# A decoder layer on one core: split weights 128 bytes into longer tiles, decay ahead of the last head's sums, the MLP norm applied late

## The chip, the core and the metric

The kernel runs on one core of a Trainium2 chip. A core has a matmul engine (PE; its weight loads are shown beside it as PEld), a vector engine (DVE), a scalar engine (ACT), a general engine (POOL) and a sync engine (SP) that here only issues transfers. Every engine takes its own instructions strictly in the order in which the program issues them to it, and waits on semaphores for the others. Data lies in SBUF (128 partitions); matmuls write PSUM, of which this kernel has eight buffers of 128x512 fp32. The metric is the device time of one launch in microseconds (us).

## The reference

One layer of an autoregressive decoder for 512 tokens of width 1024, all in fp32:

```python
h = rmsnorm(x, ln1);  hq, hk, hv, hr, ha, hatt, hgate = split(h @ w_in)
log_a = log_sigmoid(ha @ w_a2 + b_a) / 16                 # decay of the gated linear attention
o = gla_mixer(hq, hk, hv, log_a)                          # 4 heads, chunks of 64
y_gla = (norm(o) * gla_gn * silu(hr)) @ w_o_gla
o_att = merge of 3 dilated attention groups, 4 heads each # softmax over the groups' sums
x = x + (sigmoid(g_gla) * y_gla + sigmoid(g_att) * (o_att @ w_o_attn)) @ w_out
x = x + square(relu(rmsnorm(x, ln2) @ w_mlp1)) @ w_mlp2   # 1024 -> 4096 -> 1024
x = x + sigmoid(rmsnorm(x, ln3) @ w_pg) * (p @ w_pp)
return rmsnorm(x, ln_f)
```

## The kernel before

**Split operands.** A matmul runs in the rounded type fp32r, one pass. To keep fp32 precision, every operand is split into `hi` (rounded, written by ACT) and `lo` (the rest, `w - hi`, written by DVE), and a product becomes three matmuls: hi·hi, hi·lo, lo·hi. A weight arrives by DMA as a raw tile of 128x1024 (pool `wst`, 6 buffers), ACT writes its `hi` (L226) and DVE its `lo` (L221) into the pool `wsp` (5 and 4 buffers); `fetch` keeps this two or three operands ahead of the matmuls. Everything else of size 128x512 lies in one arena `ar` of `NU` = 69 tiles, `ur` when of type fp32r and `u` otherwise. All tiles of `wst`, `wsp` and `ar` have sizes that are multiples of 512 bytes, and all slices used as matmul operands begin at multiples of 512 bytes in their tile.

**Seven-product groups.** Most projections (23 groups of 512 output columns, `strassen`) are done by a scheme of seven products in place of eight on 2x2 blocks: a stage per product, 24 matmuls with 256 moving columns each. The weight combinations S1 to S4 come by DMA with accumulation (POOL) and two DVE sums (L206, L212). In groups of kind `quad` the weights are the stationary operand, in `quadt` the moving one. The other weights (kinds `fm`, `tm`, `half`) are used with 512 moving columns. Per group, four results are finished by an ACT copy at the block's beginning and a DVE addition at its end.

**An order by hand.** PE's stream sets the order. `run` issues matmuls in pieces of eight and calls `step` after each. `step` takes one closure of the list `later` (finishing work, splits), and, each time `pace` moving columns have gone by, resumes one generator of the list `side`, of which the first two take turns (`WAYS` = 2). `drain` runs both lists empty with no matmuls of the main stream between.

**Where the change touches.**

- Behind the group `v0`, `pace` is set to 2560; `side` gets `pv(0)` to `pv(3)` (the weighted sums of the attention heads) and behind them `decay()` (four small products, Abs, Exp, Ln on ACT, a subtraction L817 and a prefix scan L818 on DVE for each head). They run beside the groups `gq`, `gk`, `gv0`; then `drain()`, then the linear attention `gla(0)`, `gla(1)` beside the four `oa` weights.
- Ahead of the MLP, `rms_gen(acc1, norm2, 6, 2)` waits six steps, sums squares over partitions with four one-column matmuls (L377), takes the inverse root on POOL (L364, L365), makes a diagonal matrix of it (L390), splits that, and spreads it over partitions by two matmuls (L396, L397). The result `norm2[1]` is multiplied into each hidden block together with the relu (L1167), ahead of the square (L1176).
- Each half of the second MLP product ends with four additions from PSUM into `xx` (L1226); `normed` then makes the split operands of the last norm and its sum of squares. Behind them, `pp` and `pg` run with tokens on the output partitions.
- The last token tile of `pg1` is done in two halves of 256 columns, each followed by `gated`: sigmoid (L1267), product (L1268), sum (L1269), sum of squares (L1270); `scale_out` and `put` write the output.

Of the kernel before, what the change touches and what calls it, by code (L numbers as in the profile page):

```python
# [11 lines left out]
F32R = mybir.dt.float32r  # L12
I32 = mybir.dt.int32
AF = mybir.ActivationFunctionType
OP = mybir.AluOpType
# [4 lines left out]
P = 128  # L20
T = 512
D = 1024
KC = D // P
EPS = 1e-6
# [14 lines left out]
QUADS = ("quad", "quadt")  # L39
# [54 lines left out]
UNITS = weight_units()  # L94
# [32 lines left out]
C_LN2, C_LN3, C_BA, C_GN, C_LN1, C_LO, C_N = 0, 8, 16, 20, 28, 36, 38  # L127
W0, W12 = 384, 256

NU, NW, PIECE, WAYS = 69, 5, 8, 2  # L130

NRAW = 6

NWARM = 8

# [2 lines left out]
def block_kernel(ctx, tc, xT, ws, pT, wts, wha, wa2, vec, lnf, rel, onehot, ident_d, mask_d, out):  # L138
# [13 lines left out]
    def u32(name="u"):  # L152
        return ar.tile([P, T], F32, tag="u", name=name)
# [4 lines left out]
    def mmt():  # L158
        return mm.tile([P, T], F32, tag="mm", name="mmt")
# [19 lines left out]
    def drain():  # L179
        while side or later:  # L180
            step()
# [20 lines left out]
    def sums(i):  # L202
# [7 lines left out]
        elif what == "S4":  # L210
            w = raw[f"{q}.S4"] = raw[f"{q}.S2"]
            V.tensor_tensor(w, w, raw[f"{q}.A12"], op=OP.add)  # L212

    def fetch(upto):

        while done[0] < min(upto, len(OPERANDS) - 1):
            i = done[0] = done[0] + 1
            if i >= 0:
                w, hi = ready[OPERANDS[i]]
                lo = wsp.tile([P, 1024], F32R, tag="lo", name="lo", bufs=NW - 1)  # L220
                V.tensor_tensor(lo, w, hi.bitcast(F32), op=OP.subtract)  # L221
                ready[OPERANDS[i]] = (hi, lo)
            if 0 <= i + 1 < len(OPERANDS):
                w = raw[OPERANDS[i + 1]]
                hi = wsp.tile([P, 1024], F32R, tag="hi", name="hi", bufs=NW)
                S.activation(hi, w, AF.Copy)  # L226
                ready[OPERANDS[i + 1]] = (w, hi)
            if 0 <= i + 2 < len(OPERANDS):
                sums(i + 2)
            if 0 <= i + 3 < len(OPERANDS):  # L230
                prepare(i + 3)
# [5 lines left out]
    def run(mms, n=PIECE, shared=False):  # L237
        for i in range(0, len(mms), n):
            for o, l, r, a, b in mms[i:i + n]:
                TE.matmul(o, lhsT=l, rhs=r, start=a, stop=b, skip_group_check=shared)  # L240
            step(PIECE * r.shape[-1])
# [8 lines left out]
    def cols(t, c):  # L250
        return t[0][:, c], t[1][:, c]
# [28 lines left out]
    def halves(t):  # L280
        return slice(t * HT, (t + 1) * HT)
# [79 lines left out]
    def rsqrt(r, ms, n):  # L361

        v = st.tile([P, n], F32, tag=f"rv{n}", name="rv", bufs=4)
        V.tensor_scalar(v, ms, EPS, None, op0=OP.add)  # L364
        GP.tensor_tensor(r, v, mh[:, 0:n], op=OP.pow)  # L365
# [4 lines left out]
        S.activation(t, x, AF.Square, scale=1.0 / 32.0)  # L370
        return t

    def rms_tok(acc):

        ps = smt()
        for i in range(4):
            TE.matmul(ps[:, i:i + 1], lhsT=acc[:, i * P:(i + 1) * P], rhs=ones[:, 0:1], start=True, stop=True)  # L377
        r = const.tile([P, 4], F32, name="rtok", bufs=3)
        rsqrt(r, ps[:, 0:4], 4)
        return r  # L380

    def rms_gen(acc, res, wait=0, gap=0):

        for _ in range(wait):
            yield
        r = rms_tok(acc[0])
        for _ in range(gap):
            yield
        dg = u32()
        V.tensor_tensor(dg.rearrange("p (a b) -> p a b", a=4), ident[:, None, :].to_broadcast([P, 4, P]),  # L390
                        r[:, :, None].to_broadcast([P, 4, P]), op=OP.mult)
        dh, dl = split(dg)
        for _ in range(2 + gap):
            yield
        pb = smt()
        TE.matmul(pb, lhsT=ones_r, rhs=dh, start=True, stop=False)  # L396
        TE.matmul(pb, lhsT=ones_r, rhs=dl, start=False, stop=True)  # L397
        bc = const.tile([P, T], F32, tag="rstd", name="rstd", bufs=2)
        S.activation(bc, pb, AF.Copy)
        res += [r, bc, pb]  # L400
# [586 lines left out]
    side.append(weights())  # L987
    v0 = values("v0")
    drain()
    pace[0] = 2560  # L990
    side.extend(pv(h) for h in range(4))
    side.append(decay())
    gq = heads("gq", HD_SCALE)
    gk = heads("gk", 1.0)
    gv = [values("gv0", True)]
# [152 lines left out]
        later.extend(x1_tile(j))  # L1148
    while len(later) > 5:
        step()  # L1150
    side.append(rms_gen(acc1, norm2, 6, 2))


    hid = [None] * 32
# [4 lines left out]
    def quad(q):  # L1159


        def finish(m, t, s, ps):
            add(m, s, s, ps)

            def scale():
                o = s.rearrange("p (n t) -> p n t", n=2)
                V.scalar_tensor_tensor(out=o, in0=o, scalar=0.0,  # L1167
                                       in1=norm2[1][:, None, halves(t)].to_broadcast([P, 2, HT]),
                                       op0=OP.max, op1=OP.mult)

            def act():
                for n in range(2):
                    j = 4 * q + 2 * n + m
                    if hid[j] is None:
                        hid[j] = u32()
                    S.activation(hid[j][:, halves(t)], s[:, halves(n)], AF.Square)  # L1176

            later.extend([scale, act])

        def extra(i):  # L1180
            if i in (3, 4):
                later.append(lambda: hid_split(i - 3))

        strassen(f"m1q{q}", x1_op, finish, extra=extra if q == 7 else None)
# [6 lines left out]

    for q in range(8):
        quad(q)
        if q == 0 and not norm2:
            drain()
    for k in (2, 3):
        hid_split(k)
    drain()
# [2 lines left out]
    for sub in range(2):  # L1201
        pss = [mmt() if sub == 0 else smt() for _ in range(4)]
        for kk in range(16):
            wh, wl = weight(f"m2s{sub}.{kk}")
            mms = []
            for k in (2 * kk, 2 * kk + 1):
                xh, xl = hs.pop(k)
                for o in range(4):
                    c = slice((k % 2) * 512 + o * P, (k % 2) * 512 + (o + 1) * P)
                    mms += [(pss[o], wh[:, c], xh, k == 0, False), (pss[o], wh[:, c], xl, False, False),  # L1210
                            (pss[o], wl[:, c], xh, False, k == 31)]
            run(mms)
            for k in (2 * kk + 4, 2 * kk + 5):
                hid_split(k if k < 32 or sub else k - 32)
            if sub == 1 and kk == 8:
                for k in range(2):
                    t = u32()
                    GP.dma_start(t, pT[k * P:(k + 1) * P, :])
                    pt.append(split(t))
                for g in range(2):  # L1220
                    t = u32()
                    GP.dma_start(t, lnf[:, g * 512:(g + 1) * 512].to_broadcast([P, 512]))
                    lnb.append(t)
        for o in range(4):
            j = 4 * sub + o
            V.tensor_tensor(xx[j], xx[j], pss[o], op=OP.add)  # L1226
            normed(j, C_LN3, x2s, acc2)
    while later:
        step()
# [30 lines left out]
    sp2 = const.tile([P, 4], F32, name="sp2")  # L1260
    fr = const.tile([P, 4], F32, name="fr")

    def gated(ps, i, c, tt, col):

        n = c.stop - c.start
        sg = u32()
        S.activation(sg[:, 0:n], ps[:, 0:n], AF.Sigmoid, scale=rt3[0][:, tt:tt + 1])  # L1267
        V.tensor_tensor(sg[:, 0:n], sg[:, 0:n], pps[i][:, c], op=OP.mult)  # L1268
        V.tensor_tensor(x2t[i][:, c], x2t[i][:, c], sg[:, 0:n], op=OP.add)  # L1269
        S.activation(sg[:, 0:n], x2t[i][:, c], AF.Square, scale=1.0 / 32.0, accum_out=ss2[:, col:col + 1])  # L1270

    def evac_pg0(tt, ps):
        if len(x2t) < 8:
            drain()
        gated(ps, tt, slice(0, 512), tt, tt)
        V.tensor_scalar(sp2[:, tt:tt + 1], ss2[:, tt:tt + 1], EPS, None, op0=OP.add)
        V.tensor_tensor(x2t[tt], x2t[tt], lnb[0], op=OP.mult)

    def scale_out(tt, col):

        V.tensor_scalar(sp2[:, tt:tt + 1], ss2[:, col:col + 1], sp2[:, tt:tt + 1], None, op0=OP.add)
        GP.tensor_tensor(fr[:, tt:tt + 1], sp2[:, tt:tt + 1], mh[:, 0:1], op=OP.pow)
        o = u32()
        S.activation(o, x2t[tt], AF.Copy, scale=fr[:, tt:tt + 1])
        S.dma_start(out[tt * P:(tt + 1) * P, 0:512], o)

    def put(tt, c):
        n = c.stop - c.start
# [3 lines left out]
        SY.dma_start(out[tt * P:(tt + 1) * P, 512 + c.start:512 + c.stop], o[:, 0:n])  # L1292

    def evac_pg1(tt, ps):
        gated(ps, 4 + tt, slice(0, 512), tt, 4 + tt)
        scale_out(tt, 4 + tt)
        put(tt, slice(0, 512))

    tmaj("pg0", x2s, evac_pg0)
    tmaj("pg1", x2s, evac_pg1, tts=range(3))  # L1300
    tok = slice(3 * P, 4 * P)
    for f in range(2):
        c = slice(f * 256, (f + 1) * 256)
        ps = mmt()
        run(three(ps[:, 0:256], [(cols(x2s[k], tok), cols(ready[f"pg1.{k // 2}"], slice((k % 2) * 512 + c.start, (k % 2) * 512 + c.stop)))
                                 for k in range(KC)]))
        gated(ps, 7, c, 3, 8 + f)
        if f == 0:
            V.tensor_scalar(sp2[:, 3:4], ss2[:, 8:9], sp2[:, 3:4], None, op0=OP.add)
    scale_out(3, 9)  # L1310
    put(3, slice(256, 512))
    put(3, slice(0, 256))
# [85 lines left out]
```

## Time and profile before

| | us |
|---|---|
| median of 3 runs (989.91 to 991.78) | 990.1 |
| the profiled execution: its own time | 991.5 |
| its span, first to last instruction | 989.7 |
| PE busy in the span | 973.7 |
| DVE, ACT, POOL busy | 689.4, 520.9, 94.4 |

The profiled execution is 1.8 us longer than its span and 1.4 us longer than the median of the runs. In the profile's rows, a line number is that of the code before; names follow the program (`mmt` and `smt` are the two sets of four PSUM buffers). A matmul's reported duration (about 280 ns for 256 columns) is longer than the distance to the next one, since they are pipelined; what a matmul costs is read from a stretch of the chain: time divided by count.

### The profile page before, as it was taken

What the parts mean: (1) busy time and instruction counts of PE and PEld (TensorE: products, weight loads), DVE (VectorE), ACT (ScalarE), POOL (GpSimd) and SP (SyncE); (2) the same over time, 40 slices, a digit from 0 to 9 for tenths busy, and PEclk for the clock granted to TensorE, in tenths of its full rate; (3) what the DMA queues carried; (4) which work ended last, traced back from release to release, by engine and by line L of the source; (5) the groups of instructions that cost most, each with busy time, mean ns of one, the idle gap of its engine ahead of it and who ended that gap; (6) DMA issues with size and microseconds to landing.
All of it is one profiled execution on the core that took longest, in us unless ns stands there. A gap on an engine that the chain in (4) does not pass through costs nothing.

```text
span 989.7 us, 15873 instructions
## 1 busy us (share of the span) xinstructions
PE 973.7 (98%) x6372; PEld 889.3 (90%) x6372; DVE 689.4 (70%) x966; ACT 520.9 (53%) x875; POOL 94.4 (10%) x136
## 2 busy tenths in 40 slices
PE   9999999999998999999999999999999999999996
PEld 7788999999996999999988889999998888888885
DVE  7777579676579669977955697788778445653554
ACT  7335546445575667565733446555665335442633
POOL 0230011320010021013010001010000000000000
PEclk9999999999999999999999999999999999999999
DMA  8473564974264545455636426656544332523102
GB/s 308 126 205 100 128 147 112 266 202 115 80 157 131 160 98 149 121 146 171 171 92 206 126 46 164 177 131 169 154 145 131 104 96 77 167 88 106 43 1 85
DMA packets 40026, 133.63 MB, mean 135 GB/s; under 512 B 5203, under 2 KB 6815, under 8 KB 39952
## 3 DMA queue, kind: packets, MB, share of 16 engines
q1 hardware_dynamic: 27504, 92.51, 28.5%
q0 software_dynamic: 10720, 36.96, 18.4%
q10 hardware_dynamic: 1728, 3.15, 0.8%
q8 instruction: 50, 0.82, 0.3%
q14 instruction: 24, 0.20, 0.1%
HBM read 126.26 MB, written 8.17 MB: 136 GB/s over the span
## 4 chain that ended last, share of the span: by engine, by line
PE 92%; DVE 3%; issue 2%; ACT 1%; POOL 0%; POOLq 0%; DVEq 0%; ACTq 0%
PE mmt L240 73%; PE smt L240 9%; PE smt L829 1%; DVE lo L221 1%; PE smt L769 1%; PE smt L695 1%; PE mmt L454 1%; PE mmt L453 1%; PE mmt L455 1%; PE smt L875 1%; DVE u L818 0%; PE smt L877 0%; PE smt L428 0%; PE smt L665 0%; PE smt L786 0%
## 5 line engine op out<-in xcount | busy, mean ns | idle before, releaser
L240 PE MATMUL mmt<-ur,hi 128*128 128x256 f32 (+1 forms) x2784 | 608.5, 314 | 1.8 <-ACT u L1002 1.5
L240 PEld LDWEIGHTS mmt<-ur,hi 128*128 128x128 f32 x2784 | 459.9, 191 | 34.3 <-issue 1.9
L240 PE MATMUL mmt<-ur,lo 128*128 128x256 f32 (+1 forms) x1392 | 437.4, 314 | 0.5 <-DVE lo L221 0.5
L221 DVE TENSOR_TENSOR lo<-w,hi 128x1024 fp32r<-128x1024 f32 x236 | 286.2, 1220 | 119.6 <-PE mmt L240 64.2
L226 ACT ACTIVATE hi<-w 128x1024 fp32r<-128x1024 f32 x236 | 246.8, 1053 | 137.1 <-issue 64.0
L240 PEld LDWEIGHTS mmt<-ur,lo 128*128 128x128 f32 x1392 | 266.0, 191 | 16.3 <-DVE lo L221 0.7
L240 PE MATMUL mmt<-hi,ur 128*128 128x256 f32 (+1 forms) x736 | 154.5, 306 | 0.0
L337 ACT ACTIVATE ur<-u 128x512 fp32r<-128x512 f32 x136 | 79.9, 621 | 95.2 <-DVE u L1066 30.9
L240 PEld LDWEIGHTS mmt<-hi,ur 128*128 128x128 f32 x736 | 119.4, 191 | 5.6
L240 PE MATMUL mmt<-lo,ur 128*128 128x256 f32 (+1 forms) x368 | 112.4, 305 | 0.0
L345 DVE TENSOR_TENSOR ur<-u,ur 128x512 fp32r<-128x512 f32 x135 | 89.0, 686 | 20.3 <-ACT ur L337 19.7
L330 DVE TENSOR_TENSOR u<-u,mmt 128x512 f32<-128x512 f32 (+1 forms) x92 | 58.0, 654 | 39.0 <-PE mmt L240 37.4
L240 PE MATMUL smt<-ur,hi 128*128 128x512 f32 x272 | 83.7, 389 | 0.0
L312 ACT ACTIVATE u<-mmt 128x512 f32<-128x512 f32 x92 | 54.4, 592 | 49.7 <-PE mmt L240 49.7
L240 PEld LDWEIGHTS mmt<-lo,ur 128*128 128x128 f32 x368 | 70.2, 191 | 2.7
L240 PEld LDWEIGHTS smt<-ur,hi 128*128 128x128 f32 x272 | 51.1, 188 | 10.6
L240 PE MATMUL smt<-ur,lo 128*128 128x512 f32 x136 | 53.0, 390 | 0.0
L209 POOL DMA_DIRECT2D w<-in_wts_dram x23 | 20.1, 875 | 289.8 <-DVE w L206 210.5
L1176 ACT ACTIVATE u<-u 128x256 f32<-128x256 f32 x64 | 23.0, 409 | 37.2 <-DVE u L1167 37.2
L198 POOL DMA_DIRECT2D w<-in_wts_dram x23 | 20.4, 886 | 202.4 <-DMA w<-in_wts_dram 84.6
L240 PEld LDWEIGHTS smt<-ur,lo 128*128 128x128 f32 x136 | 25.5, 188 | 5.3
L212 DVE TENSOR_TENSOR w<-w 128x1024 f32<-128x1024 f32 x23 | 28.2, 1225 | 0.8
(203 smaller groups left out, 718.2 us busy)
## 6 DMA issues: line engine op xcount, KB each, us to landing
w<-in_wts_dram SPq DMA_DIRECT2D x167, 512.0 KB, 4.0
w<-in_wts_dram POOLq DMA_DIRECT2D x46, 512.0 KB, 5.5
u<-in_xT_dram SPq DMA_DIRECT2D x8, 256.0 KB, 4.7
v_dram<-u POOLq DMA_DIRECT2D x8, 256.0 KB, 6.2
u<-v_dram POOLq DMA_DIRECT2D x8, 256.0 KB, 7.3
y_dram<-u ACTq DMA_DIRECT2D x8, 256.0 KB, 2.4
u<-y_dram POOLq DMA_DIRECT2D x8, 256.0 KB, 7.3
u<-in_xT_dram POOLq DMA_DIRECT2D x8, 256.0 KB, 8.1
```

Of the source, the lines that this page charges most:

```text
L198: GP.dma_start(w, wts[UNIT[f"{q}.A22"]], accum_op=OP.add)
L209: GP.dma_start(w, wts[UNIT[f"{q}.A21"]], accum_op=OP.add)
L212: V.tensor_tensor(w, w, raw[f"{q}.A12"], op=OP.add)
L221: V.tensor_tensor(lo, w, hi.bitcast(F32), op=OP.subtract)
L226: S.activation(hi, w, AF.Copy)
L240: TE.matmul(o, lhsT=l, rhs=r, start=a, stop=b, skip_group_check=shared)
L312: S.activation(sums[c], bank[b], AF.Copy, scale=-scale if c[0] else scale)
L330: V.tensor_tensor(out, s, ps, op=OP.subtract if m else OP.add)
L337: S.activation(hi, x, AF.Copy)
L345: V.tensor_tensor(lo, x, hi.bitcast(F32), op=OP.subtract)
L453: TE.matmul(q0ps[i], lhsT=hi[:, c], rhs=xh, start=k == 0, stop=False)
L1176: S.activation(hid[j][:, halves(t)], s[:, halves(n)], AF.Square)
```

## The change

- **Weight tiles.** `hi` and `lo` tiles are 1152 elements long instead of 1024 (4608 bytes). Operands of the seven-product groups use elements 32 to 1055, so they begin 128 bytes into the tile; the others use elements 0 to 1023.
- **Room.** The arena has 71 tiles instead of 69; the DMA scratch of the POOL queue is set to 8192 bytes (the default in the program before is 16384).
- **Decay.** The order of `side` is `pv(0)`, `pv(1)`, `pv(2)`, `decay()`, `pv(3)`, and `pace` stays at 2048 columns.
- **MLP norm.** `rms_gen` waits 30 steps instead of 6 (gap 4 instead of 2) and computes 1/(mean square + eps) with a DVE reciprocal: since relu(x·r)² = r²·relu(x)², the factor is no longer needed in the hidden blocks (L1167 becomes a maximum with 0) and is multiplied into the PSUM result behind the second product, one more DVE operation for each of the eight output tiles.
- **Last tile.** The last token tile of `pg1` is cut into 384 and 128 columns; both sigmoids are issued ahead of the first part's sum of squares. The first three output transfers of the first half go by SP's queue instead of ACT's.

```diff
-NU, NW, PIECE, WAYS = 69, 5, 8, 2
+NU, NW, PIECE, WAYS = 71, 5, 8, 2
+PAD, SHIFT = 128, 32
+LAST = 384
...
+    def split_weights(tag, i, bufs):
+
+        t = wsp.tile([P, 1024 + PAD], F32R, tag=tag, name=tag, bufs=bufs)
+        o = SHIFT if OPERANDS[i] not in UNIT or UNITS[UNIT[OPERANDS[i]]][1] in QUADS else 0
+        return t[:, o:o + 1024]
...
-                lo = wsp.tile([P, 1024], F32R, tag="lo", name="lo", bufs=NW - 1)
+                lo = split_weights("lo", i, NW - 1)
...
-                hi = wsp.tile([P, 1024], F32R, tag="hi", name="hi", bufs=NW)
+                hi = split_weights("hi", i + 1, NW)
...
-        rsqrt(r, ps[:, 0:4], 4)
+        if squared:
+            V.tensor_scalar(r, ps[:, 0:4], EPS, None, op0=OP.add)
+            V.reciprocal(r, r)
+        else:
+            rsqrt(r, ps[:, 0:4], 4)
...
-    pace[0] = 2560
-    side.extend(pv(h) for h in range(4))
-    side.append(decay())
+    side.extend([pv(0), pv(1), pv(2), decay(), pv(3)])
...
-    side.append(rms_gen(acc1, norm2, 6, 2))
+    side.append(rms_gen(acc1, norm2, 30, 4, True))
...
-            def scale():
-                o = s.rearrange("p (n t) -> p n t", n=2)
-                V.scalar_tensor_tensor(out=o, in0=o, scalar=0.0,
-                                       in1=norm2[1][:, None, halves(t)].to_broadcast([P, 2, HT]),
-                                       op0=OP.max, op1=OP.mult)
+            def positive():
+                V.tensor_scalar(s, s, 0.0, None, op0=OP.max)
...
-            V.tensor_tensor(xx[j], xx[j], pss[o], op=OP.add)
+            t = u32()
+            V.tensor_tensor(t, pss[o], norm2[1], op=OP.mult)
+            V.tensor_tensor(xx[j], xx[j], t, op=OP.add)
             normed(j, C_LN3, x2s, acc2)
...
-        S.dma_start(out[tt * P:(tt + 1) * P, 0:512], o)
+        (S if tt == 3 else SY).dma_start(out[tt * P:(tt + 1) * P, 0:512], o)
...
-    for f in range(2):
-        c = slice(f * 256, (f + 1) * 256)
-        ps = mmt()
...
-        gated(ps, 7, c, 3, 8 + f)
-        if f == 0:
-            V.tensor_scalar(sp2[:, 3:4], ss2[:, 8:9], sp2[:, 3:4], None, op0=OP.add)
+    parts, sgs = [slice(0, LAST), slice(LAST, 512)], []
+    for c in parts:
+        ps, n = mmt(), c.stop - c.start
...
+        sgs.append(gate(ps, n, 3))
+        if c.start == 0:
+            gated(sgs[0], 7, c)
+    squares(sgs[0], 7, parts[0], 8)
+    gated(sgs[1], 7, parts[1])
+    V.tensor_scalar(sp2[:, 3:4], ss2[:, 8:9], sp2[:, 3:4], None, op0=OP.add)
+    squares(sgs[1], 7, parts[1], 9)
     scale_out(3, 9)
...
-    nc = _bacc.Bacc("TRN2", target_bir_lowering=False, num_devices=1)
+    nc = _bacc.Bacc("TRN2", target_bir_lowering=False, num_devices=1, dynamic_dma_scratch_size=8192)
```

More of the change, by code (lines that the diff above doesn't have):

```diff
@@ L371, in square, with rms_tok @@
         return t
-    def rms_tok(acc):
+    def rms_tok(acc, squared=False):
         ps = smt()
@@ L378, in rms_tok, with rms_gen @@
         r = const.tile([P, 4], F32, name="rtok", bufs=3)
-        rsqrt(r, ps[:, 0:4], 4)
+        if squared:
[3 more added lines that the diff above has]
+            rsqrt(r, ps[:, 0:4], 4)
         return r
-    def rms_gen(acc, res, wait=0, gap=0):
+    def rms_gen(acc, res, wait=0, gap=0, squared=False):
         for _ in range(wait):
             yield
-        r = rms_tok(acc[0])
+        r = rms_tok(acc[0], squared)
         for _ in range(gap):
@@ L1176, in act @@
                     S.activation(hid[j][:, halves(t)], s[:, halves(n)], AF.Square)
-            later.extend([scale, act])
+            later.extend([positive, act])
         def extra(i):
@@ L1193, in block_kernel @@
         quad(q)
-        if q == 0 and not norm2:
-            drain()
     for k in (2, 3):
@@ L1261, in block_kernel, with gate, gated, squares @@
     fr = const.tile([P, 4], F32, name="fr")
-    def gated(ps, i, c, tt, col):
-        n = c.stop - c.start
+    def gate(ps, n, tt):
         sg = u32()
         S.activation(sg[:, 0:n], ps[:, 0:n], AF.Sigmoid, scale=rt3[0][:, tt:tt + 1])
+        return sg
+    def gated(sg, i, c):
+        n = c.stop - c.start
         V.tensor_tensor(sg[:, 0:n], sg[:, 0:n], pps[i][:, c], op=OP.mult)
         V.tensor_tensor(x2t[i][:, c], x2t[i][:, c], sg[:, 0:n], op=OP.add)
+    def squares(sg, i, c, col):
+        n = c.stop - c.start
         S.activation(sg[:, 0:n], x2t[i][:, c], AF.Square, scale=1.0 / 32.0, accum_out=ss2[:, col:col + 1])
+    def gated_all(ps, i, tt, col):
+        sg = gate(ps, 512, tt)
+        gated(sg, i, slice(0, 512))
+        squares(sg, i, slice(0, 512), col)
     def evac_pg0(tt, ps):
@@ L1274, in evac_pg0 @@
             drain()
-        gated(ps, tt, slice(0, 512), tt, tt)
+        gated_all(ps, tt, tt, tt)
         V.tensor_scalar(sp2[:, tt:tt + 1], ss2[:, tt:tt + 1], EPS, None, op0=OP.add)
@@ L1294, in evac_pg1 @@
     def evac_pg1(tt, ps):
-        gated(ps, 4 + tt, slice(0, 512), tt, 4 + tt)
+        gated_all(ps, 4 + tt, tt, 4 + tt)
         scale_out(tt, 4 + tt)
@@ L1301, in block_kernel @@
     tok = slice(3 * P, 4 * P)
-    for f in range(2):
-        c = slice(f * 256, (f + 1) * 256)
-        ps = mmt()
-        run(three(ps[:, 0:256], [(cols(x2s[k], tok), cols(ready[f"pg1.{k // 2}"], slice((k % 2) * 512 + c.start, (k % 2) * 512 + c.stop)))
-                                 for k in range(KC)]))
-        gated(ps, 7, c, 3, 8 + f)
-        if f == 0:
-            V.tensor_scalar(sp2[:, 3:4], ss2[:, 8:9], sp2[:, 3:4], None, op0=OP.add)
+    parts, sgs = [slice(0, LAST), slice(LAST, 512)], []
+    for c in parts:
+        ps, n = mmt(), c.stop - c.start
+        run(three(ps[:, 0:n], [(cols(x2s[k], tok), cols(ready[f"pg1.{k // 2}"], slice((k % 2) * 512 + c.start, (k % 2) * 512 + c.stop)))
+                               for k in range(KC)]))
+        sgs.append(gate(ps, n, 3))
[5 more added lines that the diff above has]
+    squares(sgs[1], 7, parts[1], 9)
     scale_out(3, 9)
```

## The prediction
> **What bounds the kernel now.** I read the page's head first, then the chain of work that ended last, in order of time.
>
> ```profile
> span 989.7 us, 15873 instructions
> PE 973.7 (98%) x6372; PEld 889.3 (90%) x6372; DVE 689.4 (70%) x966; ACT 520.9 (53%) x875; POOL 94.4 (10%) x136
> ...
> PE 92%; DVE 3%; issue 2%; ACT 1%; POOL 0%; POOLq 0%; DVEq 0%; ACTq 0%
> ```
>
> PE is the bound almost throughout: 92% of the chain is its own stream. So an edit can do two things only: make a matmul cheaper, or remove a place where the stream stops. The cost of a matmul is read in two undisturbed pieces of the chain, one with 256 moving columns (x112), one with 512 (x384):
>
> ```profile
> 441.82 13.44 PE mmt L240 x112
> ...
> 834.82 87.04 PE smt L240 x384
> ```
>
> 13.44/112 = 120.0 ns and 87.04/384 = 226.7 ns. The difference, 106.7 ns, is 256 columns, 0.417 ns each. What is left of both is the same 13.3 ns for each matmul, whatever its width. Where the stream stops is found by the busy time of each stretch:
>
> ```profile
> 216.50:293.00 76.50, 76.50 (x646) 75.98 (x646) 51.92 (x85) 44.84 (x68) 3.40 (x4) 1.00 0.50 130
> 240.00:250.00 10.00, 10.00 (x87) 10.00 (x86) 10.00 (x23) 4.02 (x6) 0.84 (x1) 1.00 0.51 107
> 300.00:325.00 25.00, 20.75 (x101) 15.75 (x100) 21.57 (x41) 15.81 (x28) 1.90 (x3) 1.00 0.41 118
> 586.00:601.00 15.00, 12.69 (x88) 11.87 (x87) 12.45 (x16) 10.85 (x16) 1.91 (x2) 0.89 0.51 133
> ```
>
> The columns are length, then busy time of PE, PEld, DVE, ACT, POOL, then the granted clock. PE is idle for 4.25 us at 300 to 325, behind the attention, and for 2.31 us at 586 to 601, ahead of the MLP, where the clock was also 0.89 in the mean, 0.11 x 15 = 1.65 us of lost work. Beside these there is the tail of some 8 us, in which no matmul runs.
>
> **Weight tiles.** A seven-product group has 7 x 24 = 168 matmuls of 256 columns, and each group does one sum at L212:
>
> ```profile
> L212 DVE TENSOR_TENSOR w<-w 128x1024 f32<-128x1024 f32 x23 | 28.2, 1225 | 0.8
> ```
>
> 23 x 168 = 3864 matmuls get a weight operand that begins 128 bytes later relative to the arena's tiles. They are 3864 x 120 ns = 464 us of the span, so 1 ns in each is worth 3.9 us. The count of instructions and the bytes do not change. What can the offset touch? Only the 13.3 ns. The trace has operands of the weight pool and of the arena, as stationary and as moving ones, at every multiple of 512 bytes, and the excess is the same in all undisturbed pieces; it has no pair of fp32r operands with another relative offset at this width. So the cost is bounded from below by -13.3 ns (all of the excess gone: -51.5 us) and from above by the dearest short piece of matmuls that I find:
>
> ```profile
> 925.50 1.38 PE mmt L240 x6
> ```
>
> 230 ns against 226.7: +3.3 ns, +12.8 us. One row speaks for something between:
>
> ```profile
> L240 PEld LDWEIGHTS mmt<-ur,hi 128*128 128x128 f32 x2784 | 459.9, 191 | 34.3 <-issue 1.9
> L240 PEld LDWEIGHTS smt<-ur,hi 128*128 128x128 f32 x272 | 51.1, 188 | 10.6
> ```
>
> A weight load takes 191 ns where most matmuls are narrow, and 188 ns where all are wide. If 3 ns of the narrow step were of that kind and went, it would be 11.6 us. But the wide step has the quick load and still its 13.3 ns. Nearest to the rows, where buffer and slice never mattered, is no change; I take 0 and keep -51.5 and +12.8 as ends.
>
> The Trainium skill bears on this twice, in "TensorE: Matmul & The Clock Gate". Under "Step-by-step: what each phase is for" it gives the array two independent read ports and says that loading the next weights does not take read bandwidth from the running matmul; by that an offset changes nothing. Under "Back-to-back issue gap" it states, for a warm isolated matmul, 2.5 ns beyond the columns; the 13.3 ns here differ from that, so by that page something in this stream is dearer than it need be, and what it would be worth is a rival below.
>
> **Decay.** Behind the last group, DVE does this (first and last of four pairs, and the weight that PE waits for):
>
> ```profile
> 295.20 0.69 DVE L817 TENSOR_TENSOR u<-u 128x512 f32<-128x512 f32 x1
> 295.92 1.23 DVE L818 TENSOR_TENSOR_SCAN u<-u 128x512 f32<-128x512 f32 x1
> ...
> 302.64 1.22 DVE L818 TENSOR_TENSOR_SCAN u<-u 128x512 f32<-128x512 f32 x1
> ...
> 305.75 1.22 DVE L221 TENSOR_TENSOR lo<-w,hi 128x1024 fp32r<-128x1024 f32 x1
> ```
>
> The reason is a count. `pv` needs 8 resumptions each, `decay` 21: 53. Three groups have 63 pieces of 2048 columns, which at a pace of 2560 resume 50 times; so the last of `decay` is left to `drain`, where four pairs of some 1.8 us fall on DVE at once, with the last splits, and behind them the first work of `gla`. At 2048 there are 63 resumptions for 53. `pv(0)`/`pv(1)` take 16, `pv(2)`/`decay` 16, `decay`/`pv(3)` 16, the rest of `decay` 5: done ten pieces, some 10 us, ahead of the end. `decay` issues no transfer, so no DMA queue sees the move. So the 7.2 us leave the crowded place. PE's 4.25 us there are a lower count, since in each of some six gaps a matmul's modelled end hides 0.15 to 0.25 us; I put the stops at 5.2 and let 0.3 remain: -4.9. What is late next: the denser pace. In 216.5 to 293 DVE is busy for 51.92 of 76.5 us and has room for 7.2 more, but at 240 to 250 it is full, and with every resumption 20% sooner PE's transposes come sooner behind DVE's scaling. PE stands still nowhere there today; I charge +0.7, with 0 and +2.5 (a third of what the decay cost at the end) as ends. Sum -4.2, between -5.4 and -2.
>
> **MLP norm.** Today's chain:
>
> ```profile
> 593.46 0.15 DVE L364 TENSOR_SCALAR rv<-smt 128x4 f32<-128x4 f32 x1
> 594.77 0.69 DVE L390 TENSOR_TENSOR u<-ident,rtok 128x512 f32<-128x512 f32 x1 [1.16 <-POOL rtok L365]
> 596.22 0.69 DVE L345 TENSOR_TENSOR ur<-u,ur 128x512 fp32r<-128x512 f32 x1 [0.75 <-ACT ur L337]
> ```
>
> PE waits for it at L396 and L397. With 24 more steps of wait, and gaps of 4, some 40 pieces of 0.96 us lie between, and POOL is out of it. That frees the idle 2.31 us but for about 0.5 that belongs to the splits of x ahead of it (DVE, unchanged), the 1.65 us of clock that the stop cost, and 0.3 of hidden ends: -3.8. L1167 gets no dearer and hides beside PE. The price comes at the other end, where the factor is applied:
>
> ```profile
> 919.86 2.73 DVE L1226 TENSOR_TENSOR u<-u,smt 128x512 f32<-128x512 f32 x4 [7.56 <-PE smt L240]
> ...
> 927.56 1.22 DVE L221 TENSOR_TENSOR lo<-w,hi 128x1024 fp32r<-128x1024 f32 x1
> ...
> 943.70 0.69 DVE L1268 TENSOR_TENSOR u<-u 128x512 f32<-128x512 f32 x1 [4.36 <-ACT u L1267]
> 944.43 0.69 DVE L1269 TENSOR_TENSOR u<-u 128x512 f32<-128x512 f32 x1
> ...
> 929.21 0.39 PE L240 MATMUL mmt<-lo,ur 128*128 128x512 f32 x1
> ```
>
> DVE runs without a break from 919.86 to 928.78, when the `lo` of the second `pp` weight is written; PE uses it first at 929.21. Now four dependent pairs, 0.73 + 0.60 each by the rows of L1268 and L1269, take 5.3 us in place of 2.7. The `lo` lands at 931.4, and PE stands for 931.4 - 929.2 = +2.2 us. Bounds: +1.4 (if the adds' own wait for PE hides some) and +3.8 (if the stop also costs clock, 1.65, as the one at 596 did). The same four behind the first half cost nothing: DVE has free time beside 32 wide matmuls per pair of blocks. Sum -1.6, between -2.6 and 0.
>
> **Last tile.** The old order keeps ACT waiting: the second sigmoid (982.37) stands behind the first sum of squares.
>
> ```profile
> 258.82 0.45 PE smt L775 x4
> ...
> 980.11 0.37 ACTq L1285 DMA_DIRECT2D out_dram<-u  x1
> 980.53 0.47 ACT L1267 ACTIVATE u<-mmt,rtok 128x256 f32<-128x256 f32 x1 [0.45 <-ACT u L1284]
> 982.37 0.46 ACT L1267 ACTIVATE u<-mmt,rtok 128x256 f32<-128x256 f32 x1
> 984.32 0.21 DVE L1281 TENSOR_SCALAR sp<-ss,sp 128x1 f32<-128x1 f32 x1 [0.58 <-ACT u L1270]
> ```
>
> PE: 48 x 120 = 5.76 us become 24 x (384 x 0.417 + 13.3 = 173) + 24 x P. No fp32r matmul of 128 columns is in the trace; other 128-column ones take 0.45/4 = 112 ns. With 112, 6.85 us, PE ends 1.1 us later. The transfer issued by ACT at 980.11 goes to SP, whose queue is empty there, and frees ACT 0.4 us sooner for the first sigmoid. Then sigmoid, product and sum of 128 columns, and both sums of squares on ACT, bring L1281 to about 984.2, against 984.32: 0. Ends: P as a 256-column one, 120 (+0.2), or as a wide one, 227 (+2.8).
>
> **Room.** Two more arena tiles and less DMA scratch meet no wait on PE's list: 0.
>
> Sum: -4.2 - 1.6 = -5.8 on the profiled 991.5, that is 985.7; the median stands 1.4 lower, so 990.1 - 5.8 = **984.3**. Its own range by the ends, not all at once: 981 to 988.
>
> **Rivals.**
> - A, the narrow step gets its quick load, 3 ns: 984.3 - 11.6 = 972.7. For: 191 against 188. Against: the wide step.
> - B, the excess comes from both operands lying in step, and most of it goes. By rows up to -51.5; at three quarters, 984.3 - 38.6 = 946. For: it is the same at every width, as a collision of each load with the stream would be. Against: it never varies with the buffer. (By the 2.5 ns of the page named above it would be 3864 x 10.8 = 41.7 us, 943.)
> - C, the change does not do what it says for the decay: the stop is `gla`'s own DVE work, or moves into the denser stretch: 984.3 + 4.2 = 988.5.
> - D, slower: the offset puts the weights' reads out of step and each narrow matmul costs 3.3 ns more: 984.3 + 12.8 = 997. It decides from 5.8/3864 = 1.5 ns on. For: nothing but the lack of such a row.
>
> **How the numbers follow.** Forecast 0.46, A 0.27, B 0.13, C 0.07, D 0.07. The forecast, C and A with the room between them and a little beyond give the range 964 to 989; B and D, 0.20, are left out. Faster or slower by over 0.2% (2 us, about what a measurement of this kernel can tell from no change) comes to: faster 0.46 + 0.27 + 0.13 and a little of C, 0.88; same, most of C, 0.06; slower, most of D, 0.06.
>
> **What would show it.** Divide a long piece of narrow matmuls by its count: 120.0 means forecast, 117 A, 107 to 113 B, over 121.5 D. PE's idle time at 300 to 325 should fall under 1 us, and none over 2.5 appear in 216 to 293 (else C). No stop and a clock of 1.00 around 596; a new stop of about 2 us where `pp`'s second weight is first used, on L221. I am wrong if the offset acts, if that new stop takes the clock with it, or if 128-column fp32r matmuls are dear.

## The result and the profile after

| | before | after |
|---|---|---|
| median of 4 runs each, us | 990.94 (989.91 to 994.52) | 979.48 (978.87 to 979.73) |
| the profiled execution: time, span | 991.5, 989.7 | 979.7, 977.9 |
| PE busy | 973.7 | 968.3 |

The ratio is 0.9877 (95% interval 0.9851 to 0.9904): faster by 11.5 us, twice the 5.8 forecast and inside the range given. The head of the page of the kernel after, and its line on the chain of work that ended last, by engine:

```profile
span 977.9 us, 15875 instructions
...
PE 968.3 (99%) x6372; PEld 885.3 (91%) x6372; DVE 685.9 (70%) x975; ACT 522.6 (53%) x875; POOL 94.6 (10%) x135
...
PE 96%; DVE 2%; issue 1%; DMA 1%; ACT 0%; SPq 0%; POOLq 0%; POOL 0%; DVEq 0%
```

PE has as many instructions as before and is busy 5.4 us less, so matmuls themselves became cheaper; and its share of the chain rose from 92 to 96%, so stops went as well. First the matmuls: pieces of the same chain, in order of time (start, length, count), inside stretches that nothing disturbs. The pitch of a matmul, from its start to the start of the next, is length divided by count.

```profile
109.96 30.12 PE mmt L250 x251
...
639.99 60.04 PE mmt L250 x506
...
823.40 87.04 PE smt L250 x384
```

The narrow matmuls (256 moving columns) cost 30.12/251 = 120.0 ns around 110 us, as before, but 60.04/506 = 118.66 ns around 640. The wide ones (512) stay at 87.04/384 = 226.7. Over all pairs of narrow matmuls that follow each other undisturbed the mean fell from 119.86 to 118.84 ns; times 3864 that is 3.9 us. The weight loads of this group, 191 ns in the mean before, fell too (the costliest groups; busy, mean ns, idle before):

```profile
L250 PEld LDWEIGHTS mmt<-ur,hi 128*128 128x128 f32 x2784 | 455.6, 188 | 32.2 <-issue 1.9
```

That is the 188 ns that the loads of the wide matmuls have had all along. Experiment 1 will show that the shorter loads are not what shortens the pitch.

Then the stops, in the busy time of four stretches (length, then busy time and count of PE, PEld, DVE, ACT, POOL, then granted clock, DMA share, GB/s). The first is the prediction's, ended at 290 in place of 293, the second is the same as there; the others are the places of the two old stops, moved with the stream.

```profile
216.50:290.00 73.50, 73.50 (x624) 72.93 (x623) 55.59 (x91) 45.13 (x67) 4.16 (x5) 1.00 0.47 116
240.00:250.00 10.00, 10.00 (x84) 9.82 (x83) 9.97 (x21) 5.14 (x9) 0.84 (x1) 1.00 0.38 78
295.00:320.00 25.00, 25.00 (x129) 20.58 (x128) 20.88 (x40) 16.31 (x29) 2.83 (x4) 1.00 0.66 183
575.00:600.00 25.00, 24.18 (x199) 23.57 (x198) 24.71 (x33) 16.70 (x27) 1.72 (x2) 1.00 0.62 162
```

PE never stands still behind the attention any more (25.00 of 25.00, against 20.75 of 25 before), nor in the denser stretch ahead of it. Ahead of the MLP 0.82 us of idle time remain, at full clock. DVE is all but full there (24.71 of 25), and both of PE's waits, 0.50 and 0.32 us, are for a `lo` that DVE writes behind its other splits. Some 0.5 us of that kind was foreseen.

The new stop foreseen at the second `pp` weight did not come. The timeline of the kernel after, DVE and PE at that place:

```profile
899.65 1.23 DVE L231 TENSOR_TENSOR lo<-w,hi 128x1024 fp32r<-128x1024 f32 x1 [4.27 <-PE smt L250]
...
917.79 0.40 PE L250 MATMUL mmt<-lo,ur 128*128 128x512 f32 x1
...
918.21 0.69 DVE L1101 TENSOR_TENSOR u<-u 128x512 f32<-128x512 f32 x1
...
918.81 1.22 DVE L231 TENSOR_TENSOR lo<-w,hi 128x1024 fp32r<-128x1024 f32 x1
```

The longer chain of additions (L1234, L1235) and the norm's work do end only at 918.9, and a `lo` does stand behind them. But PE uses the `lo` of the second `pp` weight at 917.79, ahead of that `lo`'s beginning. So the `lo` in the queue is that of a later weight. Counted from the end, where the last eight belong to `pg0` and `pg1`, it is the first one of `pg0`; the one needed here is the last that was written before the additions began, at 899.65 (in the kernel before, at 911.07). Aligned by matmul, the two kernels' streams keep the same distance, within 0.05 us, from the second MLP product to the last tile.

At the end (the same timeline view):

```profile
970.68 0.28 PE L250 MATMUL mmt<-hi,ur 128*128 128x128 f32 x1
970.99 0.37 ACT L1274 ACTIVATE u<-mmt,rtok 128x128 f32<-128x128 f32 x1 [1.82 <-PE mmt L250]
971.25 0.51 ACT L1285 ACTIVATE u<-u 128x384 f32<-128x384 f32 x1
...
972.48 0.21 DVE L1301 TENSOR_SCALAR sp<-ss,sp 128x1 f32<-128x1 f32 x1 [0.34 <-ACT u L1285]
```

From the beginning of the last matmul to L1301 it is 1.80 us; before, from 981.00 to 984.32 (L1281), it was 3.32.

### The profile page after: what moved, and what is told of

It reads as the page before. It is cut to its first block, busy times and chain, and to the rows that moved or that the text cites. A ratio compares the mean times of both kernels' runs of the same rounds, so it can differ in the third digit from the quotient of the medians.

```text
span 977.9 us, 15875 instructions
## 1 busy us (share of the span) xinstructions
PE 968.3 (99%) x6372; PEld 885.3 (91%) x6372; DVE 685.9 (70%) x975; ACT 522.6 (53%) x875; POOL 94.6 (10%) x135
## 4 chain that ended last, share of the span: by engine, by line
PE 96%; DVE 2%; issue 1%; DMA 1%; ACT 0%; SPq 0%; POOLq 0%; POOL 0%; DVEq 0%
PE mmt L250 77%; PE smt L250 9%; PE smt L843 1%; PE smt L783 1%; PE smt L709 1%; PE smt L889 1%; PE mmt L468 1%; DMA u<-in_xT_dram 1%; PE mmt L469 0%; DVE lo L231 0%; PE mmt L467 0%; PE smt L891 0%; DVE ur L355 0%; PE smt L680 0%; PE smt L800 0%
## 5 line engine op out<-in xcount | busy, mean ns | idle before, releaser
L250 PEld LDWEIGHTS mmt<-ur,lo 128*128 128x128 f32 x1392 | 262.3, 188 | 16.7 <-DVE lo L231 1.2
L250 PE MATMUL mmt<-hi,ur 128*128 128x256 f32 (+3 forms) x736 | 154.8, 307 | 0.0
L250 PEld LDWEIGHTS mmt<-hi,ur 128*128 128x128 f32 x736 | 118.7, 189 | 5.4
L250 PE MATMUL mmt<-lo,ur 128*128 128x256 f32 (+3 forms) x368 | 112.9, 307 | 0.0
```

## The experiments

Two accounts stood against each other after the result. **Mine, amended:** the gain is the decay, the norm and an offset that I had put at 0. **Against it:** that the offset does nothing and the norm and the decay are worth more (the forecast's own 0 for the offset), or that the decay's stop would have gone anyhow (rival C). So each part was first undone alone, or done alone.

**1. The changed kernel without the offset.**

```diff
-PAD, SHIFT = 128, 32
+PAD, SHIFT = 128, 0
```

> The changed kernel with the offset set to 0: the weight tiles stay 4608 bytes long, all else as changed. If the offset is what lowers the narrow matmuls from 120.0 to about 118.6 ns in 19 to 20 of the 23 groups, they return to 120.0 and the time rises by 3864 x 1.35 x 20/23 = 4.5 us, to about 984. Rival: the lower step comes from the stops that are gone, or from the longer tiles; then it stays at 118.6 and the time at 979.5.

982.75 us median (982.53 to 983.22), 0.9918 of before (0.9902 to 0.9934). The chain around 640 us:

```profile
639.92 60.12 PE mmt L250 x501
```

60.12/501 = 120.0 ns. The offset is worth 982.75 - 979.48 = 3.3 us, and what it acts on is the narrow matmuls' pitch: the wide one is 226.7 ns here too, and PE is as busy as in the changed kernel at both old stops (25.00 and 24.17 of 25 us). The weight loads between 640 and 700 us:

```profile
L250 PEld LDWEIGHTS mmt<-ur,hi 128*128 128x128 f32 x334 | 51.5, 189 | 0.0
```

They take 189 ns without any offset, and the pitch is 120.0 all the same: a shorter load does not bring a shorter pitch. This kernel is also the one that the forecast added up, since the offset stood in it as 0: 982.75 us, where 984.3 was forecast.

**2. The offset alone, in the kernel before** (tiles and offset as in the change, and the smaller DMA scratch that makes room for them).

> The kernel before with the offset alone (longer tiles, and the smaller DMA scratch that makes room; 69 arena tiles). If the offset acts by itself: narrow matmuls at 118.6 in most groups, 4.5 us less than before, about 986.5, and the stops at 300 to 325 and at 586 to 601 stay. Rival: it needs the other edits; then 120.0 and the time of before.

988.1 us median (10 runs, 986.25 to 993.71), 0.9976 of before (0.996 to 0.9991): 2.4 us less by this ratio, with 0.9 to 4.0 as its interval. That cannot be told from the 3.3 that undoing costs. The chain differs, though:

```profile
639.98 60.12 PE mmt L248 x501
```

In this kernel the eight MLP groups stayed at 120.0 ns with the offset in place, while the groups from `v2` to the last gate (173 to 490 us) ran at 118.5 to 119.5; the mean over all narrow pairs is 119.4, not 118.8. The same instructions with the same offset have two pitches, and something decides which.

**3. The decay behind the last head again, at the old pace.**

```diff
-    side.extend([pv(0), pv(1), pv(2), decay(), pv(3)])
+    pace[0] = 2560
+    side.extend(pv(h) for h in range(4))
+    side.append(decay())
```

> The changed kernel with the order of the side work and the pace of 2560 as before. If the decay's scans at the end of the last group make the stop: some 5 us idle PE behind the attention again, and 979.5 + 5.2 = 984.7. Rival C of the prediction: the stop comes from the first work of the linear attention, and moving the decay did little; then within 1 us of 979.5.

983.95 us median (983.83 to 984.94), 0.9932 of before (0.9916 to 0.9948): 4.5 us lost. The stretch behind the attention:

```profile
295.00:320.00 25.00, 21.16 (x100) 16.15 (x98) 23.94 (x42) 14.15 (x27) 1.83 (x3) 1.00 0.44 136
```

PE's stop is back (3.84 us idle); its four scans run at 295 to 302 us, where the changed kernel has them at 282 to 289.

**4. The old MLP norm** (6 steps of wait, inverse root on POOL, the factor multiplied into the hidden blocks, no factor behind the second product; the `drain` that stood behind the first MLP group in case the factor was not ready is back too).

```diff
-    side.append(rms_gen(acc1, norm2, 30, 4, True))
+    side.append(rms_gen(acc1, norm2, 6, 2))
...
-            def positive():
-                V.tensor_scalar(s, s, 0.0, None, op0=OP.max)
+            def scale():
+                o = s.rearrange("p (n t) -> p n t", n=2)
+                V.scalar_tensor_tensor(out=o, in0=o, scalar=0.0,
+                                       in1=norm2[1][:, None, halves(t)].to_broadcast([P, 2, HT]),
+                                       op0=OP.max, op1=OP.mult)
```

> The changed kernel with the MLP norm as before (early, inverse root on POOL, factor in the hidden blocks, one addition per output tile). By the two traces the late norm is worth 3.0 us ahead of the MLP and costs nothing behind it: 982.5, with a stop and half clock at about 585 to 600. By the prediction's sum it would be worth only 1.6: 981.1, with an undisturbed start of pp that would then come about 2 us sooner.

980.96 us median, runs of 980.73, 980.91, 981.01 and 983.29; 0.9899 of before (0.988 to 0.9917). By the median the late norm is worth 1.5 us, by the profiled execution, which is the longest of the four, 3.6. Its row:

```profile
575.00:600.00 25.00, 22.70 (x172) 21.89 (x171) 22.12 (x30) 13.95 (x23) 2.75 (x3) 0.93 0.51 124
```

2.30 us idle, and a clock of 0.93: 0.07 x 25 = 1.75 us of clock lost, as in the profiled execution of before (0.89 over 15 us, 1.65). The three shorter runs left no trace, so that the same stop cost them no clock is not shown directly. Each run's mean granted clock agrees with it: 0.996 in the longest, 0.997 to 0.998 in the other three. The 13 runs of the kernel before beside these lie in two heaps as well, six at 989.6 to 990.6 with a mean clock of 0.997 to 0.998, seven at 991.6 to 992.7 with 0.995 to 0.997. Behind the second product nothing differs from the changed kernel.

**5. The old last tile** (two halves of 256, each gated and squared in its turn; the first transfers on ACT's queue).

> The changed kernel with the last tile as before: two column halves of 256, each gated and squared in its turn, and its first output transfer issued by ACT. The prediction's term says 0: 979.5 us, and the same span within 0.3. The comparison of the two traces says that the new split costs PE 1.07 us (24 matmuls of 384 columns at 173 ns and 24 of 128 at 111.5, for 48 of 120) and gives back 1.5 us behind the last matmul: by that this kernel is 0.4 to 0.5 us longer than the changed one, 979.9 to 980.0, with the last matmul ending 1.1 us sooner and the stretch behind it 8.7 us long, not 7.2.

979.98 us median (979.6 to 980.07); the timeline:

```profile
969.55 0.28 PE L250 MATMUL mmt<-hi,ur 128*128 128x256 f32 x1
...
972.87 0.21 DVE L1301 TENSOR_SCALAR sp<-ss,sp 128x1 f32<-128x1 f32 x1 [0.58 <-ACT u L1285]
```

PE ends 1.1 us sooner, and 3.32 us lie behind, not 1.80: by the traces the new split is worth 0.4 to 0.5 us. The medians differ by 0.5 as well, but the runs of the two kernels overlap (979.6 here, 979.73 there), so the times alone do not show it.

**6 and 7. What decides between the two pitches?** In the changed kernel `q2`, `k2` and `v1` have 120.0, `v2` changes to the shorter one at 177.8 us, just behind a 32-row transpose (L698), and most later groups have 118.5 to 118.7. So such a transpose was put into the changed kernel (behind the first product of `q2` and of the first MLP group), and into the kernel of experiment 2 (behind the first product of the second MLP group).

```diff
+            if i == 0 and name in ('q2', 'm1q0'):
+                TE.transpose(smt()[:, 0:32], ident[0:32, 0:P], ident[0:32, 0:32])
```

> The changed kernel with one transpose of 32 rows more behind the first product of two seven-product groups, q2 and the first of the MLP. Theory 1 (with the offset the narrow pitch has two steady modes, 120.0 and 118.65 ns, and a disturbance of the stream puts it into the shorter one, where it stays): q2, k2 and v1 fall from 120.0 to 118.65, v2 from 118.93 and the first MLP group from 119.06 too; 3 x 168 x 1.35 + 168 x 0.7 = 0.8 us less, and 0.2 to 0.5 us more for the two transposes: 979.0 us. Theory 2 (the pitch of a group is set by where its operands lie, and q2, k2, v1 lie otherwise): these stay at 120.0 and the time is 979.5 + 0.2 to 0.5 = 979.7 to 980.0.

979.26 us median (979.16 to 979.34), not to be told from the changed kernel's 978.87 to 979.73. The chain in `q2` and `k2`:

```profile
109.89 30.14 PE mmt L250 x254
```

118.66 where it was 120.0: the disturbance put the stream into the shorter pitch, and the whole of `k2` kept it. But `v1` was back at 119.7, in the first MLP group the extra transpose changed nothing (119.2, where the changed kernel has 119.1), and the second was at 119.3, not 118.7: a disturbance can move the stream from one pitch to the other, either way. Theory 1 holds without its "where it stays".

> The kernel before with the offset alone (as in the run of the offset alone, where the eight MLP groups stayed at 120.0 ns), and one transpose of 32 rows behind the first product of the second MLP group. Theory 1 (two modes, a disturbance selects): the second to the eighth MLP group fall to 118.65, 7 x 168 x 1.35 = 1.6 us less than the offset alone. Theory 2 (the buffers that the MLP groups meet in that kernel decide): they stay at 120.0 and the time is the same within 0.3 us but for the transpose.

```profile
639.93 60.16 PE mmt L248 x507
```

118.66, where the same kernel without the transpose had 120.0; all of the second to the eighth group have 118.6 to 118.8, 0.22 us less each. The one run (988.69, a span of 986.9) says nothing against a median of 988.1 over a scatter of 7 us. So the pitch isn't fixed by which buffers meet; the state of the stream has a part in it.

**8 to 10. Which offset, and for whom?** First the 128 bytes for every weight tile, the wide matmuls' too, then 256 and 64 bytes, one run each.

```diff
-        o = SHIFT if OPERANDS[i] not in UNIT or UNITS[UNIT[OPERANDS[i]]][1] in QUADS else 0
+        o = SHIFT
```

> The changed kernel with the 128 bytes given to every weight tile, those of the 512-column matmuls too. If the offset acts on the excess of 13.3 ns that both widths share, the wide pitch falls from 226.7 by about as much as the narrow one did, 1.2 ns in some 2300 matmuls: 2.7 us less. If what it changes exists only at 256 columns, where a weight load has 120 ns of room and not 227, the wide pitch stays at 226.7 and the time at 979.5.

989.16 us, almost as long as before. The chain:

```profile
639.99 60.04 PE mmt L250 x506
...
829.39 89.60 PE smt L250 x384
```

Neither expectation held: the wide pitch rose, to 89.60/384 = 233.3 ns, 6.7 more. (There are 1776 such matmuls in the traces, not the 2300 that the expectation took.) That the change keeps the offset from the wide matmuls is worth 989.16 - 979.48 = 9.7 us. The narrow ones are at 118.66, now in `q2` and `k2` too (118.7 in both): another sign that what runs ahead of a group counts.

> The changed kernel with every weight tile, narrow and wide, begun 256 bytes later, not 128. With 128 bytes for all the wide pitch rose from 226.7 to 233.3 ns and the narrow one stayed at 118.65. If both follow how the two operands' addresses stand to each other within 512 bytes, another offset gives another pair of pitches: with twice the offset the narrow one should move on from 118.65 by another 1.35 (117.3; 464 us by 120, 5 us less) and the wide one by another 6.7 (240.0; 2300 of them, 15 us more). If any offset does the same, 118.65 and 233.3 stay and the time is that of 128 bytes for all, 989.2.

```profile
639.97 60.12 PE mmt L250 x501
...
826.55 87.04 PE smt L250 x384
```

120.0 and 226.7, and 982.78 us: as with no offset at all (982.75). Nothing of what I had written came about. 256 bytes act as 0 does, and as every multiple of 512 did before.

> The same with 64 bytes. If the pitch grows with the offset: narrow 119.3, wide 230.0, 985 us. If any offset does the same: 118.65, 233.3 and 989.2. If 64 bytes are too few to part the two operands: 120.0 and 226.7, as without an offset, 982.7.

```profile
109.92 30.15 PE mmt L250 x266
...
346.60 13.20 PE mmt L250 x112
...
639.91 60.18 PE mmt L250 x531
...
816.43 89.60 PE smt L250 x384
```

Again none of the three, and a surprise: the wide pitch is 233.3, as with 128 bytes, but the narrow one is 60.18/531 = 113.3 ns in some groups (`q2` and `k2` at 110 us among them) and 13.20/112 = 117.9 in others, 115.2 in the mean, and the kernel takes 975.58 us in spite of its dearer wide matmuls.

**11. The new pace, with the old order.**

```diff
-    side.extend([pv(0), pv(1), pv(2), decay(), pv(3)])
+    side.extend(pv(h) for h in range(4))
+    side.append(decay())
```

> The changed kernel with the decay behind the last head again (the old order), but at the new pace of 2048. By the prediction's count (53 resumptions needed, 63 to be had) the pace alone brings the decay in ahead of the end of the last group: the stop at the attention's end stays away, 979.5 and a span of 977.9. If it is the order that counts, because two sums at a time are taken in turn and the decay, alone at the end, meets the last products, the stop is back in part or in whole: 980.5 to 984.

979.05 us (one run), and no stop:

```profile
295.00:320.00 25.00, 25.00 (x124) 20.19 (x124) 20.77 (x41) 16.71 (x30) 2.83 (x4) 1.00 0.65 177
```

The scans run at 282 to 290 us, as in the changed kernel. The count of resumptions decides, not the order; the new order of `side` has no effect here that can be told.

**12. A better kernel: 64 bytes, for the narrow matmuls alone.**

```diff
-PAD, SHIFT = 128, 32
+PAD, SHIFT = 128, 16
```

> The changed kernel with 64 bytes in place of 128, for the weights of the seven-product groups alone. If the offset acts on each matmul by its own two operands, the narrow pitch is that of the run with 64 bytes for all (115.2 in the mean: 113.3 in some groups, 117.8 in others) and the wide one is back at 226.7: 979.5 - 3864 x (118.84 - 115.21) ns = 965.5 us, from the other side 975.6 - 1776 x (232.84 - 227.19) ns = 965.5. If the pitch is set by the state in which the wide matmuls leave the stream, as with 128 bytes, where unshifted wide matmuls put the first groups at 120.0, more groups stay at 117.8: 3864 x up to 2.6 ns more, up to 975. If every group falls to 113.3 it is 958.

968.13 us median (5 runs, 967.49 to 968.51), 0.9762 of before (0.9743 to 0.9781): some 11 us better than the change, whose interval ends at 0.9851.

```profile
109.92 30.15 PE mmt L250 x256
...
639.91 60.18 PE mmt L250 x531
...
812.09 87.04 PE smt L250 x384
```

The wide pitch is back at 226.7, and the MLP groups from the third on have 113.3. But `q2` and `k2`, which had 113.3 behind shifted wide matmuls, have 30.15/256 = 117.8 behind unshifted ones. The mean is 115.83, not 115.21; times 3864 that is 2.4 us, most of the 2.6 by which 965.5 was missed. In the second MLP group the pitch changes from 117.8 to 113.3 at 609.9 us, right behind a short interruption by two other matmuls (L410, L411).

## Why the prediction was right, and where it was not

| term | predicted | undone alone, medians | in the two traces |
|---|---|---|---|
| offset | 0 | -3.3 | -3.9 |
| decay | -4.9 + 0.7 | -4.5 | -4.9, no new stop |
| norm, front | -3.8 | -1.5 | -3.0 |
| norm, behind | +2.2 | | 0 |
| last tile | 0 | -0.5 | -0.45 |
| sum | -5.8 | -9.8 | -12.2 |

The medians differ by 11.5 us and the two spans by 11.8; in the traces the first large product starts 0.7 us later, inside the scatter of all traces here (21.8 to 23.5 us), which counts against the sum. The parts need not add: the offset's share depends on how the stream is disturbed, and the norm's on the clock that its stop costs.

The time lies 4.8 us below the forecast, inside the range only by the room that was kept towards rival A, whose mechanism is not what ran: that the range held is in part luck. Of the 4.8, 3.3 are the offset and 1.5 the rest, by experiment 1. The forecast's own range, 981 to 988, misses the time too, and begins lower than its ends allow: 990.1 - 5.4 - 2.6 = 982.1.

- **What bounds it.** Right: both kinds of edit that the first step allowed were at work, cheaper matmuls and fewer stops.
- **Offset: the step that failed.** "Nearest to the rows, where buffer and slice never mattered, is no change; I take 0": no row of the trace had another relative offset, so the rows could not carry the 0, as the ends -51.5 and +12.8 admitted. Measured in its place: -3.3 to -3.9, a pitch of 118.7 to 120.0 between the forecast's sign of 120.0 ns and rival A's 117. A's loads did fall from 191 to 188 ns, but the pitch fell by 1.0 ns in the mean, not 3; without the offset loads of 189 ns stood beside a pitch of 120.0, and with an offset the wide matmuls became dearer beside the same 188. So the loads' duration does not set it. Rival B's mechanism, operands lying in step, is what experiments 8 to 10 and 12 bear out best, since nothing but addresses changed there and pitches of 113.3 came, next to its 107 to 113; that it is the two operands' distance, and not the weight's own start, no run shows. At 128 bytes it is worth a tenth of what B charged. Rival D's is true of the wide matmuls, twice its price: +6.7 ns with either 64 or 128 bytes.
- **The Trainium skill on it.** "TensorE: Matmul & The Clock Gate", section "Step-by-step: what each phase is for", has two independent read ports, so that loading weights takes no read bandwidth from the running matmul. In this stream the pitch depends on where the weight operand begins, so that sentence cannot be carried over to it as "addresses do not matter"; whether it is the two reads that meet, no run here separates. The section "Back-to-back issue gap" on the same page of the Trainium skill gives its 2.5 ns for an isolated matmul, not for a stream with reloads. So the page alone did not show that this stream is dearer than it need be; the experiments did, and the nearest that they came is 113.3 - 106.7 = 6.7 ns.
- **Decay.** Right in place, reason and size: -4.9 in the trace, and experiment 11 bears out the count of 53 resumptions against 50 and 63. The +0.7 for the denser pace was not needed: PE stands nowhere from 216.5 to 290 us, though DVE is at 9.97 of 10 around 245.
- **Norm, front.** Right in place, too large: the -3.8 held 1.65 us of lost clock that was read from one execution, and about 0.8 us of idle time stayed, not 0.5. By medians it is 1.5.
- **Norm, behind: a step that failed.** The row was read rightly and the weight wrongly. The `lo` in DVE's queue behind the additions was taken for the weight that PE needs next; weights are fetched further ahead there. Set against the medians, two errors cancelled, +2.2 here and -2.3 at the front: that the -1.6 for the norm agrees with the 1.5 measured is luck.
- **Last tile.** PE's +1.1 was right (1.07; 128-column fp32r matmuls took 111.5 ns, 112 was taken). The work behind shrank by 1.52, not by the 1.1 that the 0 needs.
- **The rest.** More room and less scratch moved nothing that shows. C fell with experiment 3: the stop is the decay's.

## What to carry to other kernels

Where a matmul's pitch is a constant above its columns whatever its width, try another start address for one operand, in a run per offset and for each width apart: it moves neither instructions nor bytes, 64 bytes were worth 982.75 - 968.13 = 14.6 us where 128 were worth 3.3, and at another width the same offset was a loss. A cost that a trace cannot vary is not a zero; name it as the widest term. And when a wait is charged to an instruction behind a queue, find out for whom that instruction works before charging it.

## What the runs showed of the hardware that was not expected

All at a granted clock of 1.00, fp32r, weights reloaded for every matmul; the offset is that of the weight tile alone.

| offset, bytes | 256 columns, ns | 512 columns, ns |
|---|---|---|
| 0 | 120.0 | 226.7 |
| 64 | 113.3 or 117.8 | 233.3 |
| 128 | 118.7 or 120.0 | 233.3 |
| 256 | 120.0 | 226.7 |

Above the 0.417 ns for each column, that is 6.7, 13.3 or 20 ns in the steady cases, steps of 16 columns' time, with intermediate means (11.1 and 12.0 ns) as a second state at 64 and 128 bytes. Which state a stretch has depends on what ran ahead of it, and a single interruption can change it: one transpose of 32 rows moved seven groups from 120.0 to 118.7. What it is in the array or in the memory that makes the steps stays open, as does what an interruption must be like to move the stream the right way; offsets other than these four, and an offset of the other operand, weren't tried, so whether it is the distance between the two operands that counts, or the weight's own start, stays open too.
